# Attention stage of a two-layer trunk: compressed weights of both row blocks in one pass, one copy of c, k's rope sum on VectorE, another step order

## The chip, the core and the metric

The kernel runs on one core of one Trainium2 chip. The time is device microseconds of one execution, and the median of several runs is compared. The engines are named as the profile names them: PE (TensorE matmul; PEld its weight loads), DVE (VectorE), ACT (ScalarE), POOL (GpSimd), SP (SyncE, which here issues the transfers of the weights).

## The reference, cut

The trunk has two layers of feed-forward, mixer, feed-forward, each followed by a layer norm, on 256 rows of 1024. The mixer of layer 0 is a chunked gMLP, that of layer 1 is the sparse attention (NSA) that the change touches. There 16 heads of 64 share 4 key/value groups, and each row attends three times: to 15 compressed blocks, to selected blocks and to a window. With 256 rows all blocks are selected and the window covers all, so the last two are causal attention with keys and values of their own.

```python
q, k_c, v_c, k_s, v_s, k_w, v_w, g = split(x @ w_in)        # 1024 | 6 x 256 | 48 columns
q = rope(q); k_s = rope(k_s); k_w = rope(k_w); gates = sigmoid(g)
def compress(t, pe, w1, w2):                                 # 15 blocks of 32 rows, stride 16
    blk = concat(ch[:-1], ch[1:]) + pe
    return gelu(einsum('bnlgd,ldh->bngh', blk, w1)) @ w2
k_cmp = rope(compress(k_c, ...)); v_cmp = compress(v_c, ...)
p_cmp = masked_softmax(q . k_cmp); o_cmp = p_cmp @ v_cmp
o_slc = masked_softmax(q . k_s) @ v_s; o_win = masked_softmax(q . k_w) @ v_w
out = (gate0 * o_cmp + gate1 * o_slc + gate2 * o_win) @ w_out
```

## The kernel before, in words

Six stages run one after the other: feed-forward, gMLP, feed-forward, feed-forward, NSA, feed-forward. The 256 rows are two blocks of 128 (T = 0, 1). A matmul with weights is made of three in fp32r with operands split into a high and a low half (`mm3`, lines 272 to 276): the high half is a copy on ACT, the low half a subtraction on DVE (`split`, 305 to 307; for weights, lines 221 and 222). The weights come on SP's queue as a stream in the order in which the stages list them, into a ring of 8 pieces.

The NSA stage (`nsa`, line 560) is a list of steps, `ORDER` (line 42), run in that order by the loop at 854. Instructions that are ready can be put ahead of others when the program is built, so an engine's own order isn't always the one written. The steps, with group g from 0 to 3:

- `c T`: columns k_c and v_c of row block T; `CV T` turns them (`turn_cv`, 635) into `cT`, 64 channels on partitions, once in the lower and once, a row further, in the upper half. `c_step` (613) copies each head twice side by side for that.
- `k T`, `K T`: k_s and k_w with rope (`rope`, 542) and their transposes `kT`. `V T`: v_s and v_w. The sum at the end of rope is on POOL (line 558 for k, 553 and 556 for q).
- `B i`, `H i`: the blocks of `cT` plus `pe` (`blk`, line 657), split into `bst`, times w1 (line 668), gelu; `TK`, `KC`, `HV` make compressed keys and values.
- `Q g T`: the q of group g; `T g T`: its transpose `qT` (721, 723). `G`: the gates.
- `C g T`: compressed weights (`compressed`, 733): scores, softmax, times gate, split into `pcs`; `P T` turns them into `pct` (754).
- `S g T h`: scores against keys of both kinds and exp (`scores`, 762), times gate over sum on POOL (line 731). `A g T h`: `attend` (792) turns these weights on PE (787), splits them into `pt`, and sums the products with the values (799).
- `F T`: output projection and layer norm. `|`: memory of the first half is handed over to the second (`attention_pool`, 827).

PSUM has 8 banks: 4 with the tag "o" (scores, output), 2 with "g" (projections, `attend`), 2 with "t" (transposes and small products). A step that takes a bank waits until the one before it in this bank has been read.

Of the kernel before, what the change touches and what calls it, by code (L numbers as in the profile page):

```python
# [246 lines left out]
def tile_trunk(ctx: ExitStack, tc: tile.TileContext, plan, ins, out):  # L247
# [312 lines left out]
    def nsa(st, x, turn):  # L560
        pl = plan.stages[st]
        with tc.tile_pool(name=f"nsa{st}", bufs=1) as pool:
# [29 lines left out]
            def gate():  # L592

                for T in (0, 1):
                    f = gates[T].rearrange("p a b -> p (a b)")
                    nc.scalar.activation(f, f, AF.Exp, scale=-1.0)
                    nc.vector.tensor_scalar(f, f, 3e38, 1.0, ALU.min, ALU.add)
                    nc.vector.reciprocal(f, f)
                    if T == 0:
                        nc.vector.tensor_scalar(gates[T][:, :, 0], gates[T][:, :, 0], const[:, C_ANY:C_ANY + 1], None, ALU.mult)  # L600
# [125 lines left out]
            def scaled(p, sm, gate):  # L726

# [3 lines left out]
                nc.gpsimd.tensor_tensor(p, p, f[..., None].to_broadcast(list(p.shape)), ALU.mult)  # L731

            def compressed(g, T):

# [2 lines left out]
                for h in range(4):
                    nc.tensor.matmul(o[:, 32 * h:32 * h + 32], qT[:, h, :], kc[:, g].rearrange("p a b -> p (a b)"),
                                     start=True, stop=True)
                p = pool.tile([P, 4, 16], F32, name="pc", tag="pc", bufs=2)  # L740
                m = small.tile([P, 4], F32, name="mc", tag="mc")
                nc.vector.tensor_reduce(p, o[:, :128].rearrange("p (h i n) -> p h n i", h=4, i=2), AX.X, ALU.add)
                mask = const[:, C_MASK + 16 * T:C_MASK + 16 * T + 16]
                nc.vector.tensor_tensor(p, p, mask[:, None, :].to_broadcast([P, 4, 16]), ALU.add)
# [205 lines left out]
```

## Time and profile before

| | before |
|---|---|
| median of 3 runs | 1101.11 us (1100.66 to 1104.7) |
| the profiled execution | 1102.21 us, its span 1100.5 us |
| PE busy | 1074.0 us (98% of the span), 5437 matmuls |
| DVE, ACT, POOL busy | 724.5, 562.4, 72.1 us |
| HBM read | 208.43 MB, 190 GB/s over the span |

Busy PE means that a matmul was in flight; matmuls overlap, so it is not PE at its peak. The stage that the change touches lies between 753 and about 919 us of the span. A wait is shown with the engine and the line that ended it; a wait of an engine that is ahead of the others costs nothing.

### The profile page before, as it was taken

Reading aid. Unit: us, or ns where it says so; the run is one execution under the profiler, and the core shown is the slowest. Engines: PE = TensorE matmul, PEld = TensorE weight load, DVE = VectorE, ACT = ScalarE, POOL = GpSimd, SP = SyncE. Lnnn points to the kernel's source line nnn. Section 1 sums busy time; section 2 is a strip of 40 time slices with the busy share of each in tenths; the row PEclk is TensorE's granted clock in tenths of the full one; section 3 lists DMA queues with packets and bytes.
Section 4 is the critical chain, followed back from the end, with each engine's and each line's share of the span. In section 5 each row is a group of like instructions: output and inputs, shape, how many; then the busy total and the mean of one; then the engine's idle time right before and its main releaser. Section 6 shows DMA issues by size and latency. Waiting matters only on the chain.

```text
span 1100.5 us, 14514 instructions
## 1 busy us (share of the span) xinstructions
PE 1074.0 (98%) x5437; PEld 940.4 (85%) x5437; DVE 724.5 (66%) x971; ACT 562.4 (51%) x798; POOL 72.1 (7%) x69
## 2 busy tenths in 40 slices
PE   8999999999999999999999999999898999999997
PEld 6888888789999988888888888888787878888886
DVE  5654547768666686545476555558999888655555
ACT  6544444545444445445445544435797846544440
POOL 0000000100000010000000000002325330000000
PEclk9999999999999999999999999999999999999998
DMA  8865645867565656655457665645662117764641
GB/s 278 324 213 192 203 164 189 304 189 226 197 217 167 211 162 231 226 191 189 162 197 244 201 205 180 217 165 196 189 202 77 42 36 227 234 206 176 228 155 38
DMA packets 59686, 210.42 MB, mean 191 GB/s; under 512 B 6880, under 2 KB 7264, under 8 KB 58720
## 3 DMA queue, kind: packets, MB, share of 16 engines
q1 hardware_dynamic: 59472, 209.37, 56.8%
q8 instruction: 42, 0.69, 0.2%
q14 instruction: 28, 0.23, 0.1%
q0 software_dynamic: 144, 0.13, 0.0%
HBM read 208.43 MB, written 1.05 MB: 190 GB/s over the span
## 4 chain that ended last, share of the span: by engine, by line
PE 87%; DVE 7%; DMA 2%; ACT 2%; issue 1%; POOL 1%; SPq 0%; DVEq 0%; ACTq 0%; POOLq 0%
PE ps_g L276 17%; PE ps_g L274 17%; PE ps_g L275 17%; PE ps_o L274 9%; PE ps_o L276 9%; PE ps_o L275 9%; PE ps_t L313 3%; DVE wlo L222 2%; DMA raw<-in_w_dram 2%; PE ps_g L799 1%; PE ps_t L501 1%; ACT whi L221 1%; PE ps_o L773 1%; PE ps_t L787 1%; DVE nm L775 1%
## 5 line engine op out<-in xcount | busy, mean ns | idle before, releaser
L222 DVE TENSOR_TENSOR wlo<-raw,whi 128x1024 fp32r<-128x1024 f32 (+2 forms) x379 | 455.6, 1208 | 196.2 <-ACT whi L221 186.8
L221 ACT ACTIVATE whi<-raw 128x1024 fp32r<-128x1024 f32 (+2 forms) x379 | 392.0, 1037 | 245.7 <-PE ps_g L276 137.9
L274 PE MATMUL ps_g<-whi,xT0h 128*128 128x512 f32 (+3 forms) x520 | 192.3, 370 | 2.8 <-ACT g L376 0.9
L274 PE MATMUL ps_g<-whi,xT1h 128*128 128x512 f32 (+3 forms) x520 | 191.7, 369 | 1.5 <-DVE rope L550 1.3
L276 PE MATMUL ps_g<-whi,xT0l 128*128 128x512 f32 (+3 forms) x520 | 191.7, 369 | 0.0
L275 PE MATMUL ps_g<-wlo,xT0h 128*128 128x512 f32 (+3 forms) x520 | 191.6, 368 | 0.0
L276 PE MATMUL ps_g<-whi,xT1l 128*128 128x512 f32 (+3 forms) x520 | 191.3, 368 | 0.0
L275 PE MATMUL ps_g<-wlo,xT1h 128*128 128x512 f32 (+3 forms) x520 | 191.2, 368 | 0.0
L274 PE MATMUL ps_o<-whi,hTh 128*128 128x512 f32 x352 | 137.0, 389 | 0.0
L275 PE MATMUL ps_o<-wlo,hTh 128*128 128x512 f32 x352 | 133.4, 379 | 0.0
L276 PE MATMUL ps_o<-whi,hTl 128*128 128x512 f32 x352 | 133.4, 379 | 0.0
L274 PEld LDWEIGHTS ps_g<-whi,xT0h 128*128 128x128 f32 x520 | 98.7, 190 | 16.5 <-ACT whi L221 1.5
L274 PEld LDWEIGHTS ps_g<-whi,xT1h 128*128 128x128 f32 x520 | 98.7, 190 | 13.2 <-issue 1.9
L275 PEld LDWEIGHTS ps_g<-wlo,xT0h 128*128 128x128 f32 x520 | 98.7, 190 | 11.8 <-DVE wlo L222 0.2
L276 PEld LDWEIGHTS ps_g<-whi,xT1l 128*128 128x128 f32 x520 | 98.6, 190 | 11.5
L276 PEld LDWEIGHTS ps_g<-whi,xT0l 128*128 128x128 f32 x520 | 98.8, 190 | 11.2
L275 PEld LDWEIGHTS ps_g<-wlo,xT1h 128*128 128x128 f32 x520 | 98.7, 190 | 11.4
L365 DVE SCALAR_TENSOR_TENSOR h<-g,ps_g 128x512 f32<-128x512 f32 (+1 forms) x48 | 30.7, 640 | 67.5 <-PE ps_g L276 63.9
L276 PEld LDWEIGHTS ps_o<-whi,hTl 128*128 128x128 f32 x352 | 66.5, 189 | 9.4
L275 PEld LDWEIGHTS ps_o<-wlo,hTh 128*128 128x128 f32 x352 | 66.7, 189 | 8.3
L274 PEld LDWEIGHTS ps_o<-whi,hTh 128*128 128x128 f32 x352 | 66.6, 189 | 8.3
L326 POOL TENSOR_TENSOR rstd<-rstd,const 128x1 f32<-128x1 f32 x14 | 13.3, 947 | 914.7 <-DVE rstd L325 914.7
(168 smaller groups left out, 1039.6 us busy)
## 6 DMA issues: line engine op xcount, KB each, us to landing
raw<-in_w_dram SPq DMA_DIRECT2D x344, 512.0 KB, 4.5
raw<-in_w_dram SPq DMA_DIRECT2D x32, 384.0 KB, 3.9
lnw<-in_ln_dram SPq DMA_DIRECT2D x6, 1024.0 KB, 7.3
glw<-in_gmln_dram SPq DMA_DIRECT2D x8, 384.0 KB, 4.3
x<-in_w_dram SPq DMA_DIRECT2D x4, 256.0 KB, 5.3
lnw<-in_xT_dram SPq DMA_DIRECT2D x4, 256.0 KB, 6.1
x<-in_x_dram SPq DMA_DIRECT2D x2, 512.0 KB, 6.7
ws<-in_ws_dram SPq DMA_DIRECT2D x1, 1024.0 KB, 7.1
```

What stands on the lines that cost most here:

```text
L221: nc.scalar.activation(hi[:, c:e], t[:, off + c:off + e], AF.Copy)
L222: nc.vector.tensor_tensor(lo[:, c:e], t[:, off + c:off + e], hi[:, c:e].bitcast(F32), ALU.subtract)
L274: nc.tensor.matmul(o, a[0], b[0], start=first, stop=False)
L275: nc.tensor.matmul(o, a[0], b[1], start=False, stop=False)
L276: nc.tensor.matmul(o, a[1], b[0], start=False, stop=last)
L313: nc.tensor.transpose(t[:, i * P:(i + 1) * P], src[:, i * P:(i + 1) * P], ident)
L326: nc.gpsimd.tensor_tensor(r, r, const[:, C_EXP:C_EXP + 1], ALU.pow)
L365: nc.vector.scalar_tensor_tensor(h, g, 0.5, u, ALU.mult, ALU.mult)
L501: nc.tensor.matmul(t[:, sl[i]], ws[:, 2 * c + i, :], n[:, sl[i]], start=True, stop=True)
L773: nc.tensor.matmul(o[:, i], qT[:, h0 + h + i, :], kT[k][:, g, :, :w], start=k == 0, stop=False)
L775: nc.vector.tensor_reduce(nm[:, h:h + n], o, AX.X, ALU.max, negate=True)
L787: nc.tensor.transpose(t[:, i * P:(i + 1) * P], x, ident)
```

## The change

The compressed weights are computed for both row blocks in one pass of `compressed(g)`, in one tile of 2 x 4 heads x 16; their scaling goes from POOL to DVE, and the high half from DVE to ACT (`split`). `pcs` alternates by group in place of by row block. `c` is kept once: `turn_cv` makes four transposes into one bank and writes `cT` in 8 copies, in an order in which `blk` reads runs of 15. The sum at the end of rope goes from POOL to DVE where the result is written twice side by side (k and the compressed k). The gates of both row blocks are computed at once, with the exp held at its written place. `blk` has two buffers, `qT` four. `c`, `k` and `v` of the second row block, and `v` of the first, use an "o" bank. The list of steps is another: `H0` stands behind `Q01`, `V` comes sooner, `Q11` stands before the `|`, `C` is one step for a group and stands ahead of its use by about a group.

```diff
 ORDER = """
-    c0 CV0 k0 c1 k1 CV1 B0 H0 B1 Q00 Q01 TK T00 K1 V0 H1 KC K0 V1 T01 G C00 S000 HV Q10 S010 C01 T10 |
-    Q11 P0 S012 A000 T11 P1 Q20 A010 C10 C11 S100 T20 A012 S110 P0 Q21 S112 A100 T21 Q30 P1 A112 S200
-    C20 A110 T30 Q31 P0 S210 C21 A200 C30 S212 P1 S300 A210 T31 C31 P0 A300 F0 S312 A212 S310 P1 A312
-    A310 F1
+    c0 CV0 k0 c1 k1 CV1 B0 Q00 Q01 H0 B1 K0 T00 V0 V1 TK K1 H1 T01 KC G Q10 C0 S000 HV Q11 S010 T10 T11 |
+    P0 C1 S012 A000 P1 Q20 A010 S100 T20 A012 S110 P0 Q21 S112 A100 T21 Q30 P1 C2 A112 S200
+    A110 T30 Q31 P0 S210 A200 T31 S212 C3 P1 S300 A210 A212 P0 S310 A300 F0 S312 P1 A310
+    A312 F1
 """.split()
-QBUF = 2
+QBUF = 4
...
         else:
-            nc.gpsimd.tensor_tensor(dst, twice(a, n), twice(b, n), ALU.add)
+            nc.vector.tensor_tensor(dst, twice(a, n), twice(b, n), ALU.add)
...
-                for T in (0, 1):
-                    f = gates[T].rearrange("p a b -> p (a b)")
-                    nc.scalar.activation(f, f, AF.Exp, scale=-1.0)
...
+                f = gates.rearrange("p t a b -> p (t a b)")
+                tc.keep_in_program_order(nc.scalar.activation(f, f, AF.Exp, scale=-1.0))
+                nc.vector.tensor_scalar(f, f, 3e38, 1.0, ALU.min, ALU.add)
+                nc.vector.reciprocal(f, f)
...
-            cT = [pa.tile([P, NKV, S + 2], F32, name=f"cT{i}", tag=f"cT{i}") for i in (0, 1)]
+            cT = pa.tile([P, 2, 8, NKV, 16], F32, name="cT", tag="cT")
...
-                t = psum("g")
+                t = psum("o" if T else "g")
                 gemm_in(t, xT[T], pl["c"], T == 1)
-                c = pa.tile([P, 8, 2, HD], F32, name="c", tag="c", bufs=2)
-                nc.scalar.activation(c, twice(t, 8), AF.Copy)
+                c = pa.tile([P, 8 * HD], F32, name="c", tag="c", bufs=2)
+                nc.scalar.activation(c, t, AF.Copy)
...
             def turn_cv(T):
+                t = psum("t")
+                for i in range(4):
+                    nc.tensor.transpose(t[:, i * P:(i + 1) * P], got["c", T][:, i * P:(i + 1) * P], ident)
                 for i in (0, 1):
-                    t = turn4(got["c", T], i)
-                    nc.scalar.activation(cT[i][:64, :, 1 + T * P:1 + T * P + P], t[:64], AF.Copy)
-                    nc.scalar.activation(cT[i][64:, :, T * P:T * P + P], t[64:], AF.Copy)
+                    ti = t[:, 2 * P * i:2 * P * (i + 1)].rearrange("p (g n m o) -> p o m g n", g=2, m=8, o=2)
+                    for a in (0, 1):
+                        for o in (0, 1):
+                            nc.scalar.activation(cT[64 * o:64 * o + 64, i, :, a::2, 8 * T:8 * T + 8],
+                                                 ti[64 * a:64 * a + 64, o], AF.Copy)
...
             def v_step(T):
-                t = psum("g")
+                t = psum("o")
...
-                    blk = pa.tile([P, 8, n60], F32, name="blk", tag="blk")
-                    s = sv[:, :, (m0 // 8):(m0 // 8) + NCMP, 0:16:2].rearrange("p g n m -> p m g n")
+                    blk = pa.tile([P, 8, n60], F32, name="blk", tag="blk", bufs=2)
+                    s = cT[:, i, :, :, m0 // 8:m0 // 8 + NCMP]
...
-            def scaled(p, sm, gate):
+            def factor(sm, gate):
                 f = small.tile(list(sm.shape), F32, name="f", tag="f")
                 nc.vector.reciprocal(f, sm)
                 nc.vector.tensor_tensor(f, f, gate, ALU.mult)
-                nc.gpsimd.tensor_tensor(p, p, f[..., None].to_broadcast(list(p.shape)), ALU.mult)
+                return f
...
-            def compressed(g, T):
+            def compressed(g):
                 o = psum("t")
+                for T in (0, 1):
+                    for h in range(4):
+                        c = P * T + 32 * h
+                        nc.tensor.matmul(o[:, c:c + 32], got["qT", g, T][:, h, :], kc[:, g].rearrange("p a b -> p (a b)"),
+                                         start=True, stop=True)
+                all8 = [P, 8, 16]
+                pc = pool.tile([P, 2, 4, 16], F32, name="pc", tag="pc", bufs=2)
+                p = pc.rearrange("p t h n -> p (t h) n")
+                m = small.tile([P, 8], F32, name="mc", tag="mc")
+                nc.vector.tensor_reduce(p, o[:, :256].rearrange("p (h i n) -> p h n i", h=8, i=2), AX.X, ALU.add)
...
+                nc.scalar.activation(p, p, AF.Exp)
+                m4 = small.tile([P, 2, 4], F32, name="mc4", tag="mc4")
+                nc.vector.tensor_reduce(m4.rearrange("p t h -> p (t h)"), p, AX.X, ALU.add)
+                f = factor(m4, gates[:, :, 4 * g:4 * g + 4, 0])
+                nc.vector.tensor_tensor(pc, pc, f[..., None].to_broadcast([P, 2, 4, 16]), ALU.mult)
+                c = pcs[g % 2].rearrange("p t h c -> p (t h) c")
+                split(c[:, :, 0:16], c[:, :, 32:48], p)
...
-                scaled(p, sm, gates[T][:, 4 * g + h0:4 * g + h0 + nh, 1:3])
+                f = factor(sm, gates[:, T, 4 * g + h0:4 * g + h0 + nh, 1:3])
+                nc.gpsimd.tensor_tensor(p, p, f[..., None].to_broadcast(list(p.shape)), ALU.mult)
```

## Rows read from the trace of the kernel before

**Rows 1.** Busy time by stretches: start and end, length, engines' busy us (instructions), clock, DMA.

```profile
600.00:700.00 100.00, 100.00 (x481) 87.62 (x480) 56.68 (x56) 49.21 (x56) 0.00 (x0) 1.00 0.60 201
753.00:786.00 33.00, 30.06 (x160) 25.96 (x159) 27.88 (x42) 21.44 (x28) 9.21 (x9) 0.97 0.74 245
...
814.00:870.00 56.00, 50.39 (x369) 43.39 (x367) 51.34 (x134) 44.31 (x141) 28.91 (x24) 1.00 0.27 83
870.00:912.00 42.00, 39.96 (x233) 32.99 (x233) 36.20 (x86) 26.67 (x78) 10.57 (x10) 1.00 0.13 38
```

**Rows 2.** Waits of PE, 746 to 925 us: us in total, times, longest.

```profile
PE ps_g L799 <- DVE pt L307: 3.8, 4, 1.2
PE ps_g L274 <- DVE rope L550: 1.8, 2, 1.3
PE ps_g L799 <- ACT pct L759: 1.8, 2, 1.2
PE ps_t L668 <- DVE gate L587: 1.5, 1, 1.5
```

**Rows 3.** Timeline of PE: start, us, instruction, idle before and what ended it.

```profile
776.63 1.04 PE L632 MATMUL ps_t<-ident,c 128*128 128x128 f32 x8
...
782.04 0.37 PE L274 MATMUL ps_g<-whi,xT1h 128*128 128x304 f32 x1 [1.26 <-DVE rope L550]
...
784.81 0.55 PE L668 MATMUL ps_t<-whi,bst 128*128 128x256 f32 x1 [1.50 <-DVE gate L587]
...
847.68 0.50 PE L799 MATMUL ps_g<-pt,vv 128*128 128x256 f32 x2 [1.11 <-DVE pt L307]
```

**Rows 4.** Timeline of DVE.

```profile
779.75 1.81 DVE L657 TENSOR_TENSOR blk<-cT,pe 128x480 f32<-128x480 f32 x1
...
782.94 1.72 DVE L307 TENSOR_TENSOR bst<-blk,bst 128x480 fp32r<-128x480 f32 x1
...
784.70 0.97 DVE L657 TENSOR_TENSOR blk<-cT,pe 128x480 f32<-128x480 f32 x1
...
821.81 2.78 DVE L222 TENSOR_TENSOR wlo<-raw,whi 128x1024 fp32r<-128x1024 f32 x1
...
845.28 1.75 DVE L751 CAST pcs<-pc 128x64 fp32r<-128x64 f32 x1
```

**Rows 5.** Timeline of POOL.

```profile
779.52 1.28 POOL L558 TENSOR_TENSOR k<-rope,rope 128x512 f32<-128x512 f32 x1 [8.14 <-DVE rope L550]
781.97 2.17 POOL L558 TENSOR_TENSOR k<-rope,rope 128x512 f32<-128x512 f32 x1 [1.17 <-DVE rope L550]
...
845.08 1.90 POOL L731 TENSOR_TENSOR p<-p,f 128x1024 f32<-128x1024 f32 x1
```

**Rows 6.** Busy time by stretches, as rows 1: the clock.

```profile
784.00:788.00 4.00, 3.19 (x16) 3.22 (x17) 3.97 (x11) 1.61 (x4) 1.15 (x3) 0.57 0.44 135
```

**Rows 7.** DVE groups, 753 to 912 us: busy us, mean ns of one | idle before.

```profile
L657 DVE TENSOR_TENSOR blk<-cT,pe 128x480 f32<-128x480 f32 x4 | 5.2, 1308 | 0.0
L751 DVE CAST pcs<-pc 128x64 fp32r<-128x64 f32 x8 | 5.1, 638 | 1.0 <-POOL pc L731 0.9
...
L742 DVE TENSOR_REDUCE pc<-ps_t 128x64 f32<-128x128 f32 x8 | 2.3, 287 | 0.9 <-PE ps_t L738 0.7
...
L744 DVE TENSOR_TENSOR pc<-pc,const 128x64 f32<-128x64 f32 x8 | 1.8, 219 | 0.1
...
L222 DVE TENSOR_TENSOR wlo<-raw,whi 128x608 fp32r<-128x608 f32 x1 | 0.8, 792 | 0.2 <-ACT whi L221 0.2
```

**Rows 8.** Instructions on the tile pc alone: DVE, ACT, POOL busy us (instructions), clock, DMA.

```profile
753.00:912.00 159.00, 17.26 (x56) 2.04 (x8) 2.36 (x8) 0.99 0.39 124
```

**Rows 9.** ACT groups, 753 to 912 us.

```profile
L674 ACT ACT_TABLE_LOAD x2 | 2.6, 1283 | 0.0
...
L638 ACT ACTIVATE cT<-ps_t 64x512 f32<-64x512 f32 x4 | 2.4, 590 | 0.8 <-PE ps_t L632 0.7
```

**Rows 10.** Timeline of ACT.

```profile
824.83 0.26 ACT L747 ACTIVATE pc<-pc 128x64 f32<-128x64 f32 x1 [1.94 <-DVE pc L746]
```

More of the change, by code (lines that the diff above doesn't have):

```diff
@@ L570, in nsa @@
             kc = pool.tile([P, NKV, 2, 16], F32R, name="kc", tag="kc")
-            gates = [pool.tile([P, NH, 3], F32, name=f"gate{T}", tag=f"gate{T}") for T in (0, 1)]
+            gates = pool.tile([P, 2, NH, 3], F32, name="gate", tag="gate")
             got = {}
@@ L586, in q_step @@
                 if g == 0:
-                    nc.vector.tensor_copy(gates[T].rearrange("p a b -> p (a b)"), t[:, :48])
+                    nc.vector.tensor_copy(gates[:, T].rearrange("p a b -> p (a b)"), t[:, :48])
                 q = pool.tile([P, 4, 2, HD], F32R, name="q", tag="q", bufs=2)
@@ L592, in gate @@
             def gate():
[L594 to L600 removed]
+                f = gates.rearrange("p t a b -> p (t a b)")
+                tc.keep_in_program_order(nc.scalar.activation(f, f, AF.Exp, scale=-1.0))
+                nc.vector.tensor_scalar(f, f, 3e38, 1.0, ALU.min, ALU.add)
+                nc.vector.reciprocal(f, f)
+                nc.vector.tensor_scalar(gates[:, 0, :, 0], gates[:, 0, :, 0], const[:, C_ANY:C_ANY + 1], None, ALU.mult)
             pools = ExitStack()
@@ L614, in c_step @@
                 turn[T](xT)
-                t = psum("g")
+                t = psum("o" if T else "g")
                 gemm_in(t, xT[T], pl["c"], T == 1)
-                c = pa.tile([P, 8, 2, HD], F32, name="c", tag="c", bufs=2)
-                nc.scalar.activation(c, twice(t, 8), AF.Copy)
+                c = pa.tile([P, 8 * HD], F32, name="c", tag="c", bufs=2)
+                nc.scalar.activation(c, t, AF.Copy)
                 got["c", T] = c
             def k_step(T):
-                t = psum("g")
+                t = psum("o" if T else "g")
                 gemm_in(t, xT[T], pl["k"], T == 1)
@@ L712, in nsa @@
             pb = oT = None
-            pcs = [pool.tile([P, 4, 48], F32R, name=f"pcs{T}", tag=f"pcs{T}") for T in (0, 1)]
-            for T in (0, 1):
-                nc.gpsimd.memset(pcs[T].bitcast(U32), 0)
+            pcs = [pool.tile([P, 2, 4, 48], F32R, name=f"pcs{i}", tag=f"pcs{i}") for i in (0, 1)]
+            for i in (0, 1):
+                nc.gpsimd.memset(pcs[i].bitcast(U32), 0)
+            turned = [0, 0]
             def turn_q(g, T):
@@ L730, in scaled @@
                 nc.vector.tensor_tensor(f, f, gate, ALU.mult)
-                nc.gpsimd.tensor_tensor(p, p, f[..., None].to_broadcast(list(p.shape)), ALU.mult)
-            def compressed(g, T):
-                qT = got["qT", g, T]
+                return f
+            def compressed(g):
                 o = psum("t")
[L737 to L744, printed above, removed]
+                for T in (0, 1):
[8 more added lines that the diff above has]
+                nc.vector.tensor_reduce(p, o[:, :256].rearrange("p (h i n) -> p h n i", h=8, i=2), AX.X, ALU.add)
+                mask = const[:, C_MASK:C_MASK + 32].rearrange("p (t n) -> p t n", n=16)
+                nc.vector.tensor_tensor(pc, pc, mask[:, :, None, :].to_broadcast([P, 2, 4, 16]), ALU.add)
@@ L745, in compressed @@
                 nc.vector.tensor_reduce(m, p, AX.X, ALU.max)
-                nc.vector.tensor_tensor(p, p, m[:, :, None].to_broadcast([P, 4, 16]), ALU.subtract)
+                nc.vector.tensor_tensor(p, p, m[:, :, None].to_broadcast(all8), ALU.subtract)
                 nc.scalar.activation(p, p, AF.Exp)
-                nc.vector.tensor_reduce(m, p, AX.X, ALU.add)
-                scaled(p, m, gates[T][:, 4 * g:4 * g + 4, 0])
-                hi, lo = pcs[T][:, :, 0:16], pcs[T][:, :, 32:48]
@@ L754, in turn_c @@
+                split(c[:, :, 0:16], c[:, :, 32:48], p)
             def turn_c(T):
+                c = pcs[turned[T] % 2]
+                turned[T] += 1
                 t = psum("t")
                 for h in range(4):
-                    nc.tensor.transpose(t[:48, h * P:(h + 1) * P], pcs[T][:, h, :].bitcast(F32), ident)
+                    nc.tensor.transpose(t[:48, h * P:(h + 1) * P], c[:, T, h, :].bitcast(F32), ident)
                 pct = pb.tile([P, 512], F32R, name="pct", tag="pct", bufs=2)
```

4 lines of the change are left out of this document (removed).

## The prediction, made before the changed kernel was run

> **What bounds the kernel now.** First the busy time by stretches [rows 1]. Between 600 and 700 us, in a feed-forward stage, TensorE (PE) is busy in all of the 100 us with 481 matmuls, nearly all of 512 columns, so about 0.21 us for one of these: nothing can be won there. The attention stage is the only one that the diff touches; it lies between 753 us (first matmul of `c0`) and about 919 us (last of `F1`). There PE is idle for 2.9 of 33 us, 5.6 of 56 us and 2.0 of 42 us, while VectorE (DVE) is at 27.9 of 33 and 51.3 of 56. So the stage is PE work with holes in it, and the holes are DVE's doing in the main.
>
> Second, whom PE waited for in the stage [rows 2]: the low half of the turned weights, `pt` (DVE, 3.8 us in 4 waits), the turned compressed weights `pct` (1.8 in 2), a PSUM bank that rope had not read yet (1.8 in 2), and 1.5 us before `H0`. With the small ones left out that is 8.9 us in 9 waits. Matmuls are drawn about 0.16 us longer than their pace, so each wait costs that much more than it shows, 1.4 us in all.
>
> Third, why DVE was late [rows 4, 5]. `blk` at 779.75 took 1.81 us and its sister needs 0.97 with nothing on GpSimd (POOL); POOL's `k` sum ran from 779.52 to 780.80. The subtraction into `bst` at 782.94 ended at 784.66, behind POOL's next `k` sum (781.97 to 784.14). The 64-column CAST at 845.28 took 1.75 us for 0.19 of work, and ended at 847.03, with POOL's scaling of `p` (845.08 to 846.98). The 1024-column subtraction at 821.81 took 2.78 where its kind takes 1.2. A DVE instruction between SBUF tiles waits until POOL is done, and all that is queued behind it on DVE waits too.
>
> Fourth, the clock [rows 6]: between 784 and 788 us PE's granted clock was 0.57 on average, that is mostly the lower level, 1.2 GHz; right before it PE had stood in the 1.26 and the 1.50 us waits [rows 3]. In all other stretches of rows 1 it is 0.97 to 1.00. The loss is (1 - 0.57) x 4 = 1.7 us.
>
> **The change, part by part.**
>
> *c kept once.* The transposes of `c` go from 8 to 4 for a row block. Eight of them fill 1.04 us of PE [rows 3]; eight fewer in all: **-0.9 us**, on the path. ScalarE (ACT) copies half as much into `c`, and then writes `cT` in 16 copies of 64x128 instead of 8 of 64x512, which took 0.59 us each [rows 9]. Bounds for the new copy: a quarter of it (0.15) and all of it (0.59). DVE's 128-column read of PSUM over a stride of 16 elements, L742, takes 0.29 [rows 7], the nearest row; I take 0.3, so 16 x 0.3 = 4.8 against 8 x 0.59 = 4.7: nothing. They stand in the chain to `H0`: 8 copies 2.4, `blk` 0.65, the high half 0.6, the low half 0.65, together 4.3 us, while PE has `Q00` and `Q01`, 48 matmuls of 304 columns or 48 x 0.21 x 304/512 = 6.0 us. If a copy takes 0.59, the chain is 6.6 and `H0` is 0.6 late; that is the upper end. `blk` now reads runs of 15 elements in place of every 16th element: four instructions of 1.31 mean [rows 7] towards 0.65 (608 columns take 0.79 [rows 7]; 480 in proportion).
>
> [...]
>
> *k's rope sum on DVE.* Four POOL sums (1.28 us when free, 2.17 when not [rows 5]) and the small `kcr` one become DVE sums: 512 columns cost 0.69 by the 608-column row, 4 x 0.69 = 2.8, and 0.3 for `kcr`. Lower bound that; upper bound 2.8 for one if POOL holds it up, as at 821.81 [rows 4]. I take 0.69, since POOL then has only the q sums there. In return `blk` and `bst` lose their 0.84 and 1.1 us of waiting.
>
> *Banks and order, first part.* `c1`, `k1`, `V0`, `V1` take an "o" bank, free since the stage before. So `Q01` no longer waits for rope of `k1` (1.26 us [rows 3]). `H0` stands behind `Q01`; its 1.50 us wait ended with the `bst` that POOL held. With both gone the clock need not fall: 1.26 + 1.50 + 1.7 = 4.5 us. What is late next is DVE itself, busy 27.9 of 33 us before [rows 1], with 1.4 us of sums for `k1` more and some 3 us less of waits and `blk`: it follows PE's 4.5 us only in part. I take **-3.2 us** (bounds 0 and -4.5). The queue on SP: the weights of `Q0` come ahead of those of `H0`, in the order in which PE uses them already; no gain is put on that.
>
> *Compressed weights in one pass.* Before, 8 passes: 56 DVE instructions on `pc`, 17.3 us [rows 8], with L729 and L730 beside. Free of waits it would be 8 x (0.29 + 6 x 0.22) = 12.9 [rows 7]. After, 4 passes of twice the width, with the high half on ACT and the scaling on DVE in place of POOL: an element costs (792 - 219)/(608 - 64) = 1.05 ns [rows 7], so 4 x (0.42 + 6 x 0.29) = 8.6 us. DVE is relieved by 4.3 us (free) to 8.7 (as measured). PE feels that only at its waits. The CAST that POOL can hold (L751, 0.64 us mean for 0.19 of work [rows 7]) leaves DVE: the 1.11 us wait at 847.68 [rows 3] was `pt` right behind it, and one of the other three waits for `pt` has the same cause at 881 us, so 2.3 us. The longest wait for `pct`, 1.2 us [rows 2], came as ACT, in order, stood 1.94 us before the exp of `C01` [rows 10], which waited for DVE behind the 2.78 us subtraction; now `C0` lies ahead of `S000`, a step earlier than its use: 1.2 us. With 0.16 for each of these three, 4.0 us, and about a quarter of what is left there in rows 2 (3.8 + 1.8 + 0.5 - 3.5 = 2.6) from the freed DVE: 0.6. **-4.6 us.** Bounds: all waits of rows 2 outside the first part, about -7; and nothing gained but the cover lost: `Q11`, 24 matmuls of 256 columns, 24 x 0.105 = 2.5 us, now lies ahead of the attends, +2.5. ACT's new copy and the new DVE scaling wait for each other in order; queued behind the copy on ACT are exps of `S`, for which PE waits later; 4 x 0.3 us, in the upper bound.
>
> *Gates once, after H1.* ACT loaded a table five times in the stage, 1.283 each [rows 9]; exp and gelu no longer alternate, so two: -3.8 us of ACT. PE waits for ACT in rows 2 only at `pct`, so I put nothing on it. QBUF 4, two `blk` and the later `|` (it hands memory to `pct`, `pt` and `oT`, which `Q11` and `S010` don't use): no cost.
>
> **Sum.** 0.9 + 3.2 + 4.6 = 8.7. The profiled execution took 1102.2 us (span 1100.5 and 1.7 around it): 1093.5. The median of the three runs, 1101.1, is 1.1 below it: **1092.4 us**.
>
> **Rivals.** (a) *The waits move.* DVE stays at about nine tenths in 753 to 870; POOL's 12 scalings of `p` stay and can hold the new sums, the scaling and the subtractions. Then only the transposes, the clock and about 1 us remain: 0.9 + 1.7 + 1 = 3.6, 1097.5. For it: the 2.78 us row and the busy shares; against it: three of the large waits have causes that are taken out by name. To this belongs that the order does not do what it says: `Q00` ran before `H0` already (`H0` at 784.81 [rows 3]) although it was written behind, so instructions are not issued as written.
>
> (b) *Everything goes*: 0.9 + 4.8 + 7.2 (the waits of both parts with 0.16 for each), and the 1.6 us by which PE's idle time in rows 1 exceeds rows 2: 14.5, median 1086.6. For it: ACT and DVE lose work everywhere. Against it: POOL's scaling of `p` stays as it is.
>
> (c) *Slower.* A pass for both row blocks is one chain of some 2.5 us on DVE with two steps on ACT in it. If it comes to stand between the subtractions into `pt` of an attend, with no Q matmuls left to cover (the last Q ends before `S210`; `Q11` was moved out), PE waits 2.5 us in each of 4 groups, 10 us, and two of these bring the clock down as in rows 6, 3.4 us: 1102.2 - 0.9 - 3.2 + 10 + 3.4 = 1111.5, median 1110. It decides from the point at which the chain stands ahead of a `pt` in DVE's queue while POOL scales a `p`. Against it: a pass is needed only a group later (from `C3` to its `P0` there are a score and two attends), and the clock stayed at 1.00 in 814 to 912 with waits of up to 1.2 us [rows 1, 2].
>
> The Trainium skill, "TensorE: Matmul & The Clock Gate", "HAM oscillation", describes this: a PE that is idle between bursts starts each burst at half rate. The trace agrees at 784 us and shows nothing of the sort in the attends.
>
> **How the numbers follow.** Forecast 0.53 (its own range 1087 to 1096), everything 0.10 (1082 to 1087), waits move 0.26 (1096 to 1104), slower 0.11 (1106 to 1113). A measurement of this kernel tells about 0.5% from no change, 5.5 us: faster is below 1095.6. Faster: 0.53 x 0.96 + 0.10 = 0.61; slower 0.11; same 0.28. The range 1083 to 1103 leaves out the slower case and the ends of two others.
>
> **What would show it.** Right: no wait of PE near 781 and 784 us and a clock of 1.00 throughout the stage; POOL without L558; `blk` and `bst` at 0.65 to 0.8; the DVE work on `pc` near 9 us; two waits for `pt` fewer and none for `pct` above 1 us; two table loads. Wrong: `cT` copies near 0.6 us with a wait before `H0`; DVE's k sums at 1.5 us or more; PE waits for `pc`, `pct` or `pt` of 2 us in the attends; a fallen clock after 814 us; the time lost in another stage.

## The result, and the profile after the change

The changed kernel takes **1114.4 us** (median; 1114.05 to 1114.57) where the kernel before took 1101.76 us beside it: ratio **1.0109**, 95% interval 1.0097 to 1.0122. It is slower; the forecast of 1092.4 us and its range to 1103 are missed, on the side that had a chance of 0.11, and by 1.4 us beyond the upper end of that case (1113). The profiled execution has a span of 1112.8 us, 12.3 above that of before. Line numbers below are each kernel's own.

The busy times by stretches, in the columns of [rows 1], of the changed kernel:

```profile
753.00:786.00 33.00, 31.56 (x182) 27.98 (x181) 26.06 (x47) 20.47 (x36) 3.55 (x6) 1.00 0.64 207
786.00:814.00 28.00, 24.73 (x152) 21.60 (x152) 23.87 (x33) 20.42 (x33) 4.07 (x4) 0.94 0.69 223
814.00:870.00 56.00, 48.70 (x323) 42.42 (x322) 46.93 (x107) 40.38 (x121) 20.81 (x16) 0.91 0.29 87
870.00:912.00 42.00, 37.36 (x209) 31.34 (x208) 29.22 (x66) 24.91 (x83) 11.87 (x7) 0.92 0.08 26
```

The second of them in the kernel before:

```profile
786.00:814.00 28.00, 27.39 (x183) 24.49 (x182) 26.81 (x44) 24.90 (x36) 6.34 (x5) 0.97 0.61 194
```

The first part is nearly as forecast: PE is busy for 31.56 us in place of 30.06, at a clock of 1.00. From 786 us on PE does less, and the clock, 0.97 to 1.00 before, is 0.91 to 0.94. That costs up to 0.06 x 28 + 0.09 x 56 + 0.08 x 42 = 10.1 us, against 1.7 [rows 6].

DVE and ACT are busy for less than before in all four stretches; POOL too but in the last. PE isn't held by a busier engine. It waits, from 746 to 925 us (columns as in [rows 2]), for:

```profile
PE ps_t L726 <- POOL q L557: 6.0, 2, 3.3
PE ps_g L810 <- DVE sv L826: 2.4, 1, 2.4
PE ps_o L276 <- DVE wlo L223: 2.2, 1, 2.2
PE ps_g L810 <- DVE pt L308: 1.7, 3, 1.1
PE ps_o L783 <- ACT p L788: 1.1, 2, 0.9
```

In all 16.7 us in 17 waits, against 10.8 in 15. Four stand out: 3.34 us at `T11`, 2.63 at `T31`, 2.45 at an attend, 2.15 at `V0`; before, none was above 1.50. Waits and clock together are 5.9 + 8.4 us more, 0.9 us of transposes less: 13.4 against 12.3 measured. A part of the lower clock can fall into waits, where it costs nothing.

### The profile page after: what moved, and what is told of

Its sections match the earlier page's. It is cut to its first block, busy times and chain, and to the rows that moved or that the text cites. A ratio compares the mean times of both kernels' runs of the same rounds, so it can differ in the third digit from the quotient of the medians.

```text
span 1112.8 us, 14452 instructions
## 1 busy us (share of the span) xinstructions
PE 1079.2 (97%) x5429; PEld 945.2 (85%) x5429; DVE 717.8 (65%) x938; ACT 560.5 (50%) x804; POOL 60.2 (5%) x56
## 4 chain that ended last, share of the span: by engine, by line
PE 85%; DVE 7%; DMA 2%; ACT 2%; issue 2%; POOL 1%; SPq 0%; DVEq 0%; ACTq 0%; POOLq 0%
PE ps_g L277 17%; PE ps_g L275 17%; PE ps_g L276 17%; PE ps_o L277 9%; PE ps_o L276 9%; PE ps_o L275 9%; PE ps_t L314 3%; DMA raw<-in_w_dram 2%; DVE wlo L223 2%; PE ps_g L810 1%; ACT whi L222 1%; PE ps_t L502 1%; PE ps_t L798 1%; POOL p L791 1%; DVE x L344 1%
## 5 line engine op out<-in xcount | busy, mean ns | idle before, releaser
L223 DVE TENSOR_TENSOR wlo<-raw,whi 128x1024 fp32r<-128x1024 f32 (+1 forms) x379 | 454.3, 1204 | 203.0 <-ACT whi L222 193.8
L222 ACT ACTIVATE whi<-raw 128x1024 fp32r<-128x1024 f32 (+1 forms) x379 | 392.5, 1038 | 252.8 <-PE ps_g L277 134.0
L277 PE MATMUL ps_g<-whi,xT0l 128*128 128x512 f32 (+3 forms) x512 | 188.5, 368 | 0.0
L275 PE MATMUL ps_g<-whi,xT1h 128*128 128x512 f32 (+3 forms) x496 | 182.2, 367 | 0.0
L276 PE MATMUL ps_g<-wlo,xT1h 128*128 128x512 f32 (+3 forms) x496 | 181.5, 366 | 0.0
L277 PE MATMUL ps_g<-whi,xT1l 128*128 128x512 f32 (+3 forms) x496 | 181.4, 366 | 0.0
L275 PEld LDWEIGHTS ps_g<-whi,xT1h 128*128 128x128 f32 x496 | 93.9, 189 | 10.6
L277 PEld LDWEIGHTS ps_g<-whi,xT1l 128*128 128x128 f32 x496 | 93.8, 189 | 10.7
L276 PEld LDWEIGHTS ps_g<-wlo,xT1h 128*128 128x128 f32 x496 | 93.8, 189 | 10.7
L377 ACT ACTIVATE g<-ps_g 128x512 f32<-128x512 f32 (+1 forms) x48 | 26.9, 563 | 77.6 <-PE ps_g L277 76.3
```

Of the source, the lines that this page charges most:

```text
L222: nc.scalar.activation(hi[:, c:e], t[:, off + c:off + e], AF.Copy)
L223: nc.vector.tensor_tensor(lo[:, c:e], t[:, off + c:off + e], hi[:, c:e].bitcast(F32), ALU.subtract)
L275: nc.tensor.matmul(o, a[0], b[0], start=first, stop=False)
L276: nc.tensor.matmul(o, a[0], b[1], start=False, stop=False)
L277: nc.tensor.matmul(o, a[1], b[0], start=False, stop=last)
L377: nc.scalar.activation(g, src, AF.Silu)
```

## The experiments

Each time was measured beside the kernel before, and the ratio is to it, with its 95% interval. "Clock loss" is half the time that the trace's clock record has at the lower level from 745 to 945 us; with the longest wait it is read from one profiled execution, which can lie off the median (e3 3.0 us above it, e4 3.2 below, h2 2.7 above). Over all executions of the kernel before, the mean clock ran from 0.992 to 0.999. "Edits" below are all parts of the change but the list of steps; `|` is called the bar.

| kernel | ratio | longest wait of PE, us | clock loss, us |
|---|---|---|---|
| before | 1 | 1.50 | 1.7 |
| changed | 1.0109 (1.0097 to 1.0122) | 3.34 | 10.2 |
| e1, edits, old list | 1.0006 (0.9992 to 1.0021) | 1.80 | 1.7 |
| e2, before, new list | 1.0098 (1.0083 to 1.0113) | 4.04 | 8.5 |
| e3, T11 and T31 later | 1.0048 (1.0031 to 1.0065) | 2.86 | 5.1 |
| e4, old first part | 1.0081 (1.0062 to 1.0100) | 3.31 | 8.5 |
| g1, old middle | 1.0072 (1.0057 to 1.0087) | 2.63 | 5.1 |
| g2, old tail | 1.0085 (1.0069 to 1.0101) | 3.35 | 8.5 |
| f1, q on DVE | 1.0106 (1.0077 to 1.0136) | 2.72 | 10.2 |
| f2, p on DVE | 1.0068 (1.0053 to 1.0083) | 2.46 | 8.5 |
| g3, filled | 1.0082 (1.0065 to 1.0099) | 2.14 | 3.4 |
| f5, two passes, old list | 1.0005 (0.9993 to 1.0017) | 2.42 | 0 |
| h2, c once alone | 1.0044 (1.0029 to 1.0059) | 2.46 | 6.8 |
| h3, k's sum alone | 1.0039 (1.0026 to 1.0051) | 3.97 | 5.1 |
| h4, banks alone | 1.0004 (0.9993 to 1.0014) | 3.06 | 1.7 |
| i1, before, p on DVE | 1.0003 (0.9994 to 1.0012) | 1.55 | 3.4 |
| f4, a list between | 1.0012 (1.0002 to 1.0022) | 2.36 | 1.7 |
| g4, better list | 0.9988 (0.9975 to 1.0002) | 1.03 | 1.7 |
| h1, g4 with p on DVE | 0.9969 (0.9956 to 0.9981) | 1.57 | 1.7 |
| i2, h1 with T01 sooner | 0.9953 (0.9939 to 0.9967) | 1.03 | 0 |

**The theory** was that the list of steps costs the time: PE comes to a step whose input is still on its way, and the lower clock follows. **The rival** was that the one pass costs it, its chain and its scaling on DVE.

### The edits without the list, the list without the edits

e1, from the changed kernel:

```diff
-    ... B0 Q00 Q01 H0 B1 K0 T00 V0 V1 TK K1 H1 T01 KC G Q10 C0 S000 HV Q11 S010 T10 T11 |
-    P0 C1 S012 A000 P1 Q20 A010 S100 ... Q30 P1 C2 A112 S200
-    A110 T30 Q31 P0 S210 A200 T31 S212 C3 P1 S300 A210 A212 P0 S310 A300 F0 S312 P1 A310
-    A312 F1
+    ... B0 H0 B1 Q00 Q01 TK T00 K1 V0 H1 KC K0 V1 T01 G C0 S000 HV Q10 S010 T10 |
+    Q11 P0 S012 A000 T11 P1 Q20 A010 C1 S100 ... Q30 P1 A112 S200
+    C2 A110 T30 Q31 P0 S210 A200 T31 S212 C3 P1 S300 A210 P0 A300 F0 S312 A212 S310 P1 A312
+    A310 F1
```

> All edits of the change, but the list of steps of the kernel before, with C once for a group (C0 to C2 where C00, C10, C20 stood, C3 behind T31, which moves ahead of S212). Theory 'order': the new list is what costs time (TensorE stands at T11 and T31 for q that is queued on GpSimd behind the scaling of p, and each such stand brings the clock down), so without it the time is 1090 to 1102 us and at most one half-clock stretch is left in the stage. Rival 'pass': the one pass with its DVE scaling, held by GpSimd, costs it, whatever the list: 1108 to 1116 us.

e2, from the kernel before: the new list with `C` in two passes (`C11` and `C31` behind `P1`), `QBUF = 4`, and the edits of `c`.

> The kernel before with the new list (C for both row blocks, C11 and C31 behind P1, as pcs is single), with c kept once and four qT so that the memory holds it; weights in two passes, k's sum on GpSimd, gates apart, banks as before. Theory 'order': 1108 to 1118 us, with stands of 2 us and more at T11 and T31 and at least three half-clock stretches. Rival 'pass': 1097 to 1104 us.

Measured 1.0006 and 1.0098. e1 and the changed kernel differ in the list alone, and 1.03% lies between them: the list makes the loss, and the rival falls. e2 agrees, with two passes and PE standing 4.04 us at `T11`; it isn't the list alone, since `c` kept once costs 0.44% by itself (h2, below). But e1 ends where the kernel before is, just above the forecast of the theory, and not 5 us below it.

### Which part of the list

e4: the changed kernel, first part as before:

```diff
-    ... B0 Q00 Q01 H0 B1 K0 T00 V0 V1 TK K1 H1 T01 KC G Q10 C0 S000 HV Q11 S010 T10 T11 |
+    ... B0 H0 B1 Q00 Q01 TK T00 K1 V0 H1 KC K0 V1 T01 G C0 S000 HV Q10 Q11 S010 T10 T11 |
```

> The changed kernel with the old list up to HV (H0 ahead of Q00, V0 behind K1) and the new one behind it. Theory 'order': only the 2.15 us at V0 and the half clock behind it can come back (2 to 4 us), and the first-part waits of the kernel before return in part: 1110 to 1115 us, so the loss is in the second part of the list. Rival 'head': the first part is the larger share of the loss and the time falls below 1107 us.

g1: only the middle as before:

```diff
-    ... HV Q11 S010 T10 T11 | P0 C1 S012 A000 P1 Q20 A010 S100 ...
+    ... HV S010 T10 | Q11 P0 S012 A000 T11 P1 Q20 A010 C1 S100 ...
```

> The changed kernel with only the middle of the list as before: Q11 behind the bar, T11 behind A000, C1 behind A010. Theory 'cover': TensorE stands at T11 because nothing lies between Q11 and T11 that could cover q's way through VectorE, GpSimd and ScalarE; with Q11's 24 matmuls behind the bar and T11 behind A000 the 3.3 us stand and the half clock behind it go, and the 2.4 us stand at the next attend with them: 1114.4 - 6 to 9 = 1105 to 1108 us. If the loss sits in the first part or the tail instead: 1111 us or more.

g2: only the tail as before (from `C2` on, as in the diff of e1).

> The changed kernel with only the tail of the list as before (from C2 on: A112 and S200 ahead of C2, P0 and A300 ahead of F0, A212 and S310 behind F0). Theory 'cover': the 2.6 us stand at T31 stays, as T31 stands behind A200 in this list too, the waits for pt are covered by F0: 1110 to 1114 us. If the tail is the larger share of the loss: 1108 us or less.

e3: `T11` and `T31` moved, `Q11` ahead of the bar still:

```diff
-    ... Q11 S010 T10 T11 | P0 C1 S012 A000 P1 ... A200 T31 S212 C3 P1 S300 A210 ...
+    ... Q11 S010 T10 | P0 S012 A000 T11 C1 P1 ... A200 S212 T31 P1 S300 C3 A210 ...
```

> The changed kernel with T11 behind A000 (C1 behind it), T31 behind S212 and C3 behind S300; the rest of the list is the new one. Theory 'order', in its narrow form that the two places where TensorE stands at turn_q cost most: the 3.3 and the 2.6 us go, with the half clock behind each: 1114.4 - 5.9 - 3 to 5 = 1103 to 1106 us. Rival 'pass': 1112 us or more, as the wait behind the scaling of pc stays.

Against 1.0109, the first part gives back 0.28%, the middle 0.37%, the tail 0.24%, all three together (e1) 1.03%. No single place holds the loss (for the first part and the tail the intervals just touch that of the changed kernel). e3 gives 0.61%, 6.7 us, where 9 to 11 were forecast. Its two waits went (6.0 us) and half of the clock loss (5.1), but the waits moved: all of them come to 15.8 us, against 16.7, and where it stood at `T11` PE now stands at `P0`, for the `pcs` of the one pass:

```profile
826.20 0.60 PE L767 MATMUL ps_t<-ident,pcs 128*48 128x128 f32 x4 [2.86 <-DVE pcs L308]
```

In g1 the 3.3 us at `T11` went, but 4 us came, not 6 to 9, since PE now waits elsewhere:

```profile
PE ps_t L764 <- DVE pcs L305: 3.4, 2, 2.2
PE ps_g L807 <- ACT pct L766: 3.0, 2, 2.6
PE ps_o L273 <- DVE wlo L220: 2.1, 1, 2.1
```

### What PE stands for

At `T11` of the changed kernel q's low half (L557) ran on POOL behind a scaling of `p` (L791):

```profile
822.60 0.73 POOL L554 TENSOR_TENSOR rope<-rope,rope 128x256 f32<-128x256 f32 x1 [2.02 <-DVE rope L551]
823.50 2.75 POOL L791 TENSOR_TENSOR p<-p,f 128x1024 f32<-128x1024 f32 x1 [0.17 <-ACT pcs L307]
826.21 0.77 POOL L557 TENSOR_TENSOR q<-rope,q 128x256 fp32r<-128x256 f32 x1
```

f1 takes q off POOL, f2 takes `p` off it:

```diff
-            nc.gpsimd.tensor_tensor(b, a, b, ALU.add)
+            nc.vector.tensor_tensor(b, a, b, ALU.add)
...
-            nc.gpsimd.tensor_tensor(dst[:, :, 1, :], b3, dst[:, :, 0, :].bitcast(F32), ALU.subtract)
+            nc.vector.tensor_tensor(dst[:, :, 1, :], b3, dst[:, :, 0, :].bitcast(F32), ALU.subtract)
```

> The changed kernel with both GpSimd instructions of q's rope (the sum and the low half) on VectorE, the list as changed. Theory 'queue': TensorE stands at T11 and T31 because q's low half is queued on GpSimd behind the scaling of a p; so these two stands (3.3 and 2.6 us) shrink below 1 us and the half clock behind them (6.8 us each) goes: 1114.4 - 5 - 3 to 7, plus 1 to 2 us for 16 more instructions on VectorE (6.7 us of work, mostly beside): 1104 to 1109 us. Rival 'no cover': whatever is late next stands in the same places, since the list has no filler there: 1111 us or more.

```diff
-                nc.gpsimd.tensor_tensor(p, p, f[..., None].to_broadcast(list(p.shape)), ALU.mult)
+                nc.vector.tensor_tensor(p, p, f[..., None].to_broadcast(list(p.shape)), ALU.mult)
```

> The changed kernel with the twelve scalings of p on VectorE in place of GpSimd. Theory 'queue': nothing stands ahead of q on GpSimd any more and nothing holds VectorE at the scaling of pc, so the stands of 3.3, 2.6 and 2.4 us go; VectorE has 12 x 1.2 = 15 us more of work, but is no longer held up: 1102 to 1109 us. Rival 'VectorE bound': its queue becomes the bound in the attends and TensorE waits for pt: 1112 to 1120 us.

f1 changed nothing (1.0106), as its rival, no cover, had it. `T11` still stood, with DVE in POOL's place:

```profile
826.79 1.09 PE L726 MATMUL ps_t<-ident,q 128*128 128x128 f32 x4 [2.72 <-DVE q L557]
```

DVE had q's low half behind a subtraction into `pcs` that POOL held, behind `vcmp` and the low half of a weight:

```profile
821.95 2.74 POOL L791 TENSOR_TENSOR p<-p,f 128x1024 f32<-128x1024 f32 x1 [62.74 <-DVE f L734]
822.86 1.99 DVE L308 TENSOR_TENSOR pcs<-pc,pcs 128x128 fp32r<-128x128 f32 x1
824.77 0.41 DVE L308 TENSOR_TENSOR vcmp<-ps_t,vcmp 48x256 fp32r<-48x256 f32 x1
825.10 1.21 DVE L223 TENSOR_TENSOR wlo<-raw,whi 128x1024 fp32r<-128x1024 f32 x1
826.23 0.41 DVE L557 TENSOR_TENSOR q<-rope,q 128x256 fp32r<-128x256 f32 x1
```

So POOL's queue is where q was late, not why PE stood: that is the list, which has `T11` too close behind `Q11`. In e3, where `T11` comes later, PE doesn't wait there. f2 gave 0.41% back (4.5 us), and at 1110.15 us missed both of its forecasts; its wait at `T11` is 1.44 us and the one at `T31` is gone, but one of 2.46 for `pt` is new and the clock loss is nearly as high.

g3 puts needless work where PE would stand:

```diff
                 t = psum("t")
+                if T == 1 and g in (1, 3):
+                    for i in range(20):
+                        nc.tensor.matmul(t[:, :256], identr, maskr, start=True, stop=True)
```

> The changed kernel with 20 needless matmuls of 256 columns (2.2 us at the higher level) on TensorE right ahead of T11 and of T31, into the bank that the transposes then overwrite. Nothing else moves. If the half clock is a price of its own that TensorE pays for having stood, then the two half-clock stretches behind these stands (6.8 us each, in which 3.3 to 3.4 us are lost) do not come, though TensorE is free no sooner: 1107 to 1110 us. If the clock falls anyway, or the loss is the stands alone: 1113 to 1117 us.

0.27% came back, 3.0 us, though PE was free no sooner (`T11` began at 827.29 us, in the changed kernel at 827.03); that lies between its two forecasts. In 870 to 912 the clock is 1.00 where it was 0.92; in 814 to 870 it still fell (0.94), behind a wait of 1.64 us for ACT at 830 that the filling did not cover:

```profile
814.00:870.00 56.00, 51.49 (x352) 44.78 (x352) 47.89 (x110) 42.95 (x130) 21.13 (x17) 0.94 0.29 90
870.00:912.00 42.00, 38.27 (x231) 31.40 (x230) 32.50 (x67) 24.44 (x79) 12.07 (x8) 1.00 0.08 26
```

That speaks for the clock as a price of its own beside the waits, but a lower one than the record says: 6.8 us less of clock loss went with 3.0 us less of time. How large a part of the 12.3 us it is stays open: the intervals of g3 and the changed kernel just touch, and the clock did not fall at `V0` either, where nothing had been filled.

### Which edits gain

f5, e1 with the compressed weights in two passes, and so the old list word for word:

```diff
-            def compressed(g):
+            def compressed(g, T):
...
-                f = factor(m4, gates[:, :, 4 * g:4 * g + 4, 0])
-                nc.vector.tensor_tensor(pc, pc, f[..., None].to_broadcast([P, 2, 4, 16]), ALU.mult)
-                c = pcs[g % 2].rearrange("p t h c -> p (t h) c")
-                split(c[:, :, 0:16], c[:, :, 32:48], p)
+                scaled(p, m, gates[:, T, 4 * g:4 * g + 4, 0])
+                hi, lo = pcs[T][:, :, 0:16], pcs[T][:, :, 32:48]
+                nc.vector.tensor_copy(hi, p)
+                nc.vector.tensor_tensor(lo, p, hi.bitcast(F32), ALU.subtract)
```

> The old list, word for word, with all edits but the one pass: compressed weights in two passes as before (scaling on GpSimd, high half on VectorE), two qT. Against the run with all edits on the old list (1.0006 of before) this shows the pass by itself. If the one pass gains what was forecast, this is 3 to 5 us slower than that run, 1105 to 1108 us; if the pass gains nothing (a longer chain takes back what the shorter sum gives), 1099 to 1104 us; if it costs on the old list too, 1095 to 1099 us.

h2, h3, h4: one edit each in the kernel before (`c` once with `blk` in two buffers; the line of `nc.vector` in `rope` for k; `c1`, `k1`, `V0`, `V1` in "o"), as in the change's own diff.

> The kernel before with c kept once and blk in two buffers, nothing else. The prediction has 0.9 us less for 8 transposes and up to 1 us for blk, so 1100 to 1101.5 against about 1102.5 (0.998 to 0.999). If the cT copies or a shifted wait take it back: 0.9995 or more.

> The kernel before with k's rope sum on VectorE, nothing else. The prediction has 2.8 us more on VectorE and 0.84 and 1.1 us less of waiting in blk and bst: between 0.998 and 1.000. If the sums stand in VectorE's queue ahead of what TensorE waits for (Q01's bank, H0's bst): 1.001 to 1.003.

> The kernel before with c1, k1, V0 and V1 in an 'o' bank, nothing else. The prediction has Q01's wait of 1.26 us go and, with the wait behind it shorter, the half clock (1.7 us): 0.997 to 0.999. If the wait only moves to H0, behind Q01, as its producers on VectorE are no sooner done: 0.9995 to 1.0005.

1.0005 with two passes and 1.0006 with one: the pass gains nothing that is seen. `c` once alone costs 0.44% and k's sum alone 0.39%, 4.9 and 4.3 us (for k's sum more than either of its forecasts); the banks alone come out even. For h3 the trace tells how. POOL before, and POOL in h3:

```profile
819.73 0.73 POOL L556 TENSOR_TENSOR q<-rope,q 128x256 fp32r<-128x256 f32 x1 [0.79 <-ACT q L555]
820.56 2.95 POOL L731 TENSOR_TENSOR p<-p,f 128x1024 f32<-128x1024 f32 x1
```

```profile
822.68 4.47 POOL L731 TENSOR_TENSOR p<-p,f 128x1024 f32<-128x1024 f32 x1 [0.71 <-DVE f L730]
827.12 0.72 POOL L556 TENSOR_TENSOR q<-rope,q 128x256 fp32r<-128x256 f32 x1
```

and PE in h3:

```profile
827.89 1.11 PE L721 MATMUL ps_t<-ident,q 128*128 128x128 f32 x4 [3.97 <-POOL q L556]
```

Nothing was edited there; k's sums lie some 40 us earlier. Yet on POOL q's low half now comes behind `p`, not ahead of it, and PE stands 3.97 us at `T10`. So an edit of one sum can change the order in the queues of the whole stage; presumably the program's builder then takes other things to be ready first, which no run shows. "One edit alone" isn't alone: its ratio holds the edit and what comes of a new order. In h2 the largest waits are at the banks of `Q01` (2.09 us) and of a later q (2.46), and for `pcs`:

```profile
PE ps_g L274 <- DVE rope L550: 4.6, 2, 2.5
PE ps_t L762 <- DVE pcs L757: 2.1, 1, 2.1
PE ps_t L673 <- DVE bst L307: 2.0, 1, 2.0
```

In h4 the wait of `Q01` went, and that of `H0` behind it grew from 1.50 to 3.06 us; 2.76 before [rows 3] in two waits became 3.06 in one:

```profile
785.23 0.35 PE L668 MATMUL ps_t<-whi,bst 128*128 128x256 f32 x1 [3.06 <-DVE gate L587]
```

But h4 isn't the price of the banks alone either. It has a new wait at `T10`, with the clock down behind it, as q's low half took 3.37 us on POOL where 0.73 is usual:

```profile
820.42 3.37 POOL L556 TENSOR_TENSOR q<-rope,q 128x256 fp32r<-128x256 f32 x1 [0.85 <-ACT q L555]
823.85 0.66 PE L721 MATMUL ps_t<-ident,q 128*128 128x128 f32 x4 [2.37 <-POOL q L556]
```

i1 is the kernel before with only the scaling of `p` on DVE.

> The kernel before, its list and all else untouched, with only the twelve scalings of p on VectorE. If GpSimd's scaling of p is a bound by itself: 3 to 4 us faster, 0.996 to 0.998. If the gain of the best kernel so far needs its edits and list, and VectorE (51 of 56 us busy in the attends) is the bound here: 1.000 or more.

1.0003: by itself that gains nothing.

### Versions that are faster than both

f4, all edits, a list between the two:

```diff
+    ... B0 Q00 Q01 H0 B1 TK T00 K1 V0 H1 KC K0 V1 T01 G S000 C0 HV Q10 S010 T10 |
+    Q11 P0 S012 A000 P1 T11 Q20 A010 C1 S100 A012 T20 S110 P0 Q21 S112 A100 T21 Q30 P1 A112 C2 S200
+    A110 T30 Q31 P0 S210 A200 S212 T31 P1 C3 S300 A210 P0 A300 F0 S312 A212 S310 P1 A312
+    A310 F1
```

> All edits with a list between the two: H0 behind Q01 as in the new one, V0 and V1 where the old one has them, C0 behind S000, T11 behind P1 and T31 behind S212, Q11 behind the bar as in the old one. If the stands come from the places of T, V and C alone, few waits above 1.3 us are left and the edits' own gains show: 1093 to 1100 us. Rival 'the waits move': 1100 to 1106 us, with waits of 1 to 2 us for q, pcs or qT at other places.

g4, from f4:

```diff
-    ... B0 Q00 Q01 H0 B1 TK T00 ...      Q20 A010 C1 S100 ...   P1 A112 C2 S200
+    ... B0 H0 B1 Q00 Q01 TK T00 ...      Q20 C1 A010 S100 ...   P1 C2 A112 S200
```

> All edits; first part of the list as before (H0 ahead of Q00, V0 behind K1), C0 behind S000, T11 behind P1, T31 behind S212, C1 ahead of A010, C2 ahead of A112, C3 ahead of S300, the tail as before. If waits can be placed away by the list: no stand above 1.3 us, no half clock, 1094 to 1099 us. If they move, as in the list between the two (1.0012 of before): 1100 to 1105 us.

h1 is g4 with the edit of f2; i2 is h1 with `T01 V1` in place of `V1 T01`.

> The best list so far (0.9988 of before) with the twelve scalings of p on VectorE in place of GpSimd. If GpSimd's scaling, which holds VectorE's two-input instructions, is what takes the gain back: 3 to 5 us below that kernel, 1096 to 1099 us. If VectorE, with 15 us more of work, becomes the bound where the list is well covered: 1102 to 1107 us.

> The best kernel so far (0.9969) with T01 ahead of V1. If the stand of 1.5 us behind T01 (qT queued on ScalarE behind weights) and the half clock after it go: 1.5 to 3 us less, 0.994 to 0.9955. If a wait as long turns up elsewhere, as in most lists here: 0.996 to 0.999.

In f4 the waits moved (2.36 us at `V0` is the longest). g4 has none above 1.03, yet can't be told from the kernel before, as its rival forecast had it. h1 is 0.31% and i2 **0.47%** faster than before, 1097.1 us against 1102.5. i2, in the columns of [rows 1]:

```profile
786.00:814.00 28.00, 26.43 (x180) 22.42 (x179) 25.44 (x49) 22.87 (x45) 4.02 (x3) 1.00 0.76 242
814.00:870.00 56.00, 50.96 (x365) 43.74 (x365) 53.14 (x117) 44.26 (x137) 10.27 (x12) 1.00 0.21 67
870.00:912.00 42.00, 41.29 (x222) 33.21 (x222) 37.94 (x75) 24.82 (x69) 0.99 (x1) 1.00 0.25 73
```

DVE is as busy as in h1 (53.14 and 53.29 of 56), and busier than in all others, and PE is nearly full from 870 on, at a clock of 1.00 throughout. Its waits come to 8.1 us in 14, where e1 had 13.0 in 20. That the step from h1 to i2 gains by itself isn't shown: their intervals overlap.

## Why the prediction was wrong, point by point

**The step that failed is the list.** It cost 1.03%, 11.4 us (e1 against the changed kernel). The prediction priced the new order by the waits that it takes away, and put what it brings into bounds: "nothing gained but the cover lost", +2.5 us for `Q11`, and the chain of rival (c), at a chance of 0.11. That side came. `Q11` ahead of the bar cost 3.34 us at `T11`; the 2.45 us are of the kind of (c), a `pc` scaling that stands on DVE ahead of what PE needs, while POOL scales a `p`. DVE came to the second `sv`, which ended the wait, only at 844.21 us:

```profile
839.86 2.81 POOL L791 TENSOR_TENSOR p<-p,f 128x1024 f32<-128x1024 f32 x1 [0.18 <-DVE f L734]
840.83 1.98 DVE L758 TENSOR_TENSOR pc<-pc,f 128x128 f32<-128x128 f32 x1
844.21 0.43 DVE L826 TENSOR_TENSOR sv<-ps_g,sv 64x256 f32<-64x256 f32 x1
844.69 0.38 PE L810 MATMUL ps_g<-pct,vcmp 48*128 48x256 f32 x1 [2.45 <-DVE sv L826]
```

It was not the whole of (c): two of the four waits are q's turn and one the weights of `V0`, none of which the prediction named. `V0` sooner was not priced at all. Its low halves lay on DVE behind `blk` and `bst`:

```profile
788.20 0.65 DVE L661 TENSOR_TENSOR blk<-cT,pe 128x480 f32<-128x480 f32 x1
788.76 1.19 DVE L308 TENSOR_TENSOR bst<-blk,bst 128x480 fp32r<-128x480 f32 x1
789.87 1.22 DVE L223 TENSOR_TENSOR wlo<-raw,whi 128x1024 fp32r<-128x1024 f32 x1
791.14 0.80 PE L276 MATMUL ps_o<-wlo,xT0h 128*128 128x512 f32 x1 [2.15 <-DVE wlo L223]
```

**The clock.** Against (c) stood that the clock had stayed at 1.00 with waits of up to 1.2 us. That row said nothing of waits of 2.2 to 3.3 us, which the change made. By the clock rows it is the largest term, up to 8.4 us more, where the prediction took 1.7 us to come back; by g3 it is worth less than half of what the rows say. The rule that it weighed (the Trainium skill, "TensorE: Matmul & The Clock Gate", "HAM oscillation") was taken to hold at 784 us and not in the attends. The trace of the changed kernel agrees with it there too: its clock fell at 791, 829, 846 and 883 us, right behind its four long waits. That it does not follow from the length of a wait alone is shown in the last section.

**Sizes of single edits**, by rows of the changed kernel (busy us, mean ns of one):

```profile
L643 ACT ACTIVATE cT<-ps_t 64x128 f32<-64x128 f32 x16 | 4.3, 272 | 0.9 <-PE ps_t L638 0.7
L559 DVE TENSOR_TENSOR k<-rope,rope 128x512 f32<-128x512 f32 x4 | 2.7, 686 | 0.0
L661 DVE TENSOR_TENSOR blk<-cT,pe 128x480 f32<-128x480 f32 x4 | 2.6, 653 | 0.0
L758 DVE TENSOR_TENSOR pc<-pc,f 128x128 f32<-128x128 f32 x4 | 2.8, 707 | 0.0
L308 DVE TENSOR_TENSOR pcs<-pc,pcs 128x128 fp32r<-128x128 f32 x4 | 2.8, 710 | 0.4 <-ACT pcs L307 0.4
L678 ACT ACT_TABLE_LOAD x2 | 2.6, 1283 | 0.0
```

- `cT` copies: 0.27 us, forecast 0.3; k's sum 0.69 and `blk` 0.65, as forecast. Right in size, with no gain in time: alone, `c` once and k's sum were slower.
- First part, -3.2: it came nearly whole, and was lost right behind. The same matmuls, all up to the end of `Q01` and `H0`, are done 3.7 us sooner, where 4.1 were forecast with the transposes: PE's next work began at 791.91 us before (first line) and at 788.17 in the changed kernel. Then `V0` took 2.15 us and the clock fell. The banks alone (h4) gave 0; there POOL still had k's sums, and `H0` was no sooner.

```profile
791.91 0.38 PE L274 MATMUL ps_g<-whi,xT0h 128*128 128x512 f32 x1
788.17 0.60 PE L631 MATMUL ps_t<-ident,k 128*128 128x128 f32 x4
```

- One pass, -4.6: 0 (e1 against f5, within about 0.2%). The work on `pc` came to 11.85 us, not 8.6: the scaling and the subtraction took 0.71 each on average where 0.29 was put. In three passes of four they took 0.28 to 0.3; one of each took 1.98, held by POOL, as the CAST had been. One instruction that POOL can hold was traded for another.
- Gates: four table loads, not two (the sixth line above and one each at L596 and L788). Whether that cost PE time isn't shown.

**Rival (a)**, the waits move, is what the edits do on the old list: e1 is 0.06% from before, within its interval. It gave 1097.5, still with 3.6 us of gain, so even that was too hopeful.

It was wrong in the way that the prediction had named: waits of 2 us for what `pc` delays, a fallen clock after 814 us.

## What to carry to other kernels

In a stage where PE, DVE, ACT and POOL hand small pieces on, the list of steps can be worth more than the edits: here the same edits gave 1.0109, 1.0006 and, with a list that keeps each step a safe way behind what it needs, 0.9988 (0.9953 with `p` on DVE besides). For each step that a new list moves, count the PE work between the producer's last matmul and the step, and set it against the producer's whole way through the other queues as they stand, with the longest instruction that can be ahead on each; where the work is shorter, PE stands, and a fallen clock may take more. After any edit, look at the order on all queues first, also far from the edit: with a sum moved at 780 us (h3), `p` came ahead of q at 822 us and PE stood for 4 us.
